# Modulation blocks of a two-block transformer kernel: eight products on four column tiles in one run, weights in four transfers of 512 KB

## The chip, the cores and the metric

The kernel runs on one core of a Trainium2 chip. The metric is the device time of one execution in microseconds (us). A kernel is profiled once on the chip; beside that there are plain runs with no profile.

Names of engines: PE is TensorE (matrix products), PEld its weight loads, DVE is VectorE, ACT is ScalarE, POOL is GpSimd, SP is the engine that issues nearly all DMA transfers here. Each engine works its own list of instructions strictly in order.

## The reference

Two blocks are computed on a sequence of 256 tokens of width 1024 in float32. The first has two layers of attention and a gated feed-forward with a short convolution. The second has two layers as well, a latent stream (`x`) and a context stream (`ctx`), and each of its layers is modulated by vectors that come from a conditioning vector. The change concerns only how these vectors are made:

```python
s_lat = jax.nn.silu(c)[:, None, :]
s_ctx = jax.nn.silu(c_ctx)[None, None, :]
for i in range(DEPTH):                                   # DEPTH = 2
    ml = jnp.split(s_lat @ w_ada[i] + b_ada[i], 6, axis=-1)
    mc = jnp.split(s_ctx @ w_ada[i] + b_ada[i], 6, axis=-1)
    ...
    u_lat = modulate(h_lat, g_pre_mix[i], ml[0], ml[1])  # rms_norm * (1 + scale) + shift
```

`w_ada` is 2 x 1024 x 6144 in float32, 50.3 MB in all, and is read once. Both vectors go through it together.

## The kernel before

**How the work is laid out.** Most products are split in two halves of reduced precision (`whi`, `wlo` for weights, `ah`, `al` for activations), and three products take the place of one: hi by hi, hi by lo, lo by hi. A weight goes DRAM to `raw` (SP), `raw` to `whi` (ACT), `raw` minus `whi` to `wlo` (DVE or POOL), and PE uses both. The modulation is the exception: its products are plain float32 and read the loaded weight as it is.

**The lanes.** Work is recorded in three lanes with buffers of their own: the latent lane `lat`, the context lane `cx` and the side lane `sd`. A scheduler then merges them into one list per engine by its own estimate of when each instruction is ready, and packs the buffers into the on-chip memory. So the lanes interleave on PE and on SP, and the order of the source is not the order on the engine.

**The modulation.** `ada` computes layer `i`'s vectors in 12 blocks of 512 columns, 24 blocks in all. A block sums over 1024 rows, that is over eight slabs of 128 rows by 512 columns. The left operand `self.sT[:, k]` has 32 columns (two of them used: latent and context), so a product writes only 32 of the 128 rows of a PSUM bank, and the product of slab `k` goes to rows 32*(k mod 4) onward. These four places are the four column tiles. The four partial sums are added at the end: the bank is copied out (`asb`), transposed in four pieces (`adaT`) and reduced on DVE.

```python
for kb in range(0, 8, a):
    raw = (L.big if a == 2 else L.mid)([128, a, 512], name="adaw")
    nc.sync.dma_start(raw, self.plain_rows(w)(kb, a, nb * 512, 512))
    for k in range(kb, kb + a):
        j = k % 4
        nc.tensor.matmul(ps[32 * j:32 * j + 32], self.sT[:, k], raw[:, k - kb], start=k < 4, stop=k >= 4)
```

**Who calls it.** `context1` makes blocks 0 to 3 of layer 0 in the context lane and `second_block` blocks 10 and 11 of layer 1, both with `a = 2` (four transfers of 512 KB). `rest` makes blocks 4 to 11 of layer 0 and `side` blocks 0 to 9 of layer 1, both in the side lane with `a = 1` (eight transfers of 256 KB). The side lane has one PSUM bank (`PS[3]`), which holds first a block's products and then its transposes.

**What sets the order.** Each product waits only for its own slab, so the scheduler may put other lanes' products between two slabs of a block. SP issues transfers in the order of its list; a transfer into a buffer that is still in use waits, and all behind it wait too.

Of the kernel before, what the change touches and what calls it, by code (L numbers as in the profile page):

```python
# [22 lines left out]

LAT = {"big": 10, "mid": 12, "small": 24, "raw": 4, "whi": 4, "wlo": 4, "uv": 3, "gC": 1}
CTX = {"cf": 1, "big": 8, "mid": 12, "small": 24, "raw": 4, "whi": 3, "wlo": 3, "wide": 8, "gC": 1}
SIDE = {"big": 2, "mid": 6, "small": 4}
LAT_NAMED = {"AR": "raw", "BK": "big", "G": "whi", "BKt": "wlo", "lw": "big", "kn": "big", "sq": "big", "bv": "big",
             "T": "big", "TT": "big", "TTr": "big", "Y": "big", "sy": "big", "sg": "mid", "v": "mid", "uv": "uv",
             "xs": "mid", "gC": "gC"}
# [157 lines left out]
class Net:  # L187
# [10 lines left out]
    def pools(self, ctx):  # L198
# [6 lines left out]
        self.cx = Lane(self, "cx", CTX, CTX_NAMED, (("C", PS[2]), ("C", PS[2])), 512)  # L205
        self.sd = Lane(self, "sd", SIDE, {}, (("D", PS[3]), ("D", PS[3])), 512)
        self.lat.open(ctx)
# [538 lines left out]
                self.last = nc.tensor.matmul(acc[t][n], hl[:, k, c], wh[:, n], start=False, stop=en)  # L746


    def ada(self, L, i, a, blocks=range(12)):

        self.mark(f"ada{i}")
        nc, I = self.nc, self.I
        if not self.adac:
            th = L.small(16, name="ath")
            nc.scalar.activation(th[:, 0:8], self.col("c", 0, 8), AF.Tanh, scale=0.5)
            nc.scalar.activation(th[:, 8:16], self.col("cc", 0, 8), AF.Tanh, scale=0.5)
            self.sT = self.keep([128, 8, 32], F32, name="sT")
            nc.gpsimd.memset(self.sT, 0.0)  # L760
            for s, n in ((0, "c"), (1, "cc")):
                v = th[:, 8 * s:8 * s + 8]
                nc.vector.scalar_tensor_tensor(v, v, 1.0, self.col(n, 0, 8), op0=OP.add, op1=OP.mult)
                nc.vector.tensor_scalar(self.sT[:, :, s], v, 0.5, None, op0=OP.mult)
        w = I["w_ada"][i]
        if len(self.adac) == i:
            self.adac.append(self.keep([128, 2, 48], F32, name=f"adac{i}"))
        ac = self.adac[i]
        for nb in blocks:
            ps = L.pA("ada")  # L770
            for kb in range(0, 8, a):
                raw = (L.big if a == 2 else L.mid)([128, a, 512], name="adaw")
                nc.sync.dma_start(raw, self.plain_rows(w)(kb, a, nb * 512, 512))
                for k in range(kb, kb + a):
                    j = k % 4
                    nc.tensor.matmul(ps[32 * j:32 * j + 32], self.sT[:, k], raw[:, k - kb], start=k < 4, stop=k >= 4)  # L776
            sb = L.mid([128, 512], name="asb")
            nc.scalar.activation(sb, ps, AF.Copy)

            ps = L.pA("adaT")  # L780
            for c in range(4):
                nc.tensor.transpose(ps[:, c * 128:(c + 1) * 128], sb[:, c * 128:(c + 1) * 128], self.ident)
            at = ac[:, :, 4 * nb:4 * nb + 4]
            nc.vector.tensor_reduce(at, ps.rearrange("p (c j r) -> p r c j", j=4, r=32)[:, 0:2], axis=AX.X, op=OP.add)  # L784
            nc.vector.tensor_tensor(at, at, self.col(f"b_ada{i}", 4 * nb, 4)[:, None].to_broadcast([128, 2, 4]),
                                    op=OP.add)
            if nb in (3, 9):
                at, n = (8, "gpm") if nb == 3 else (32, "gpf")
                for s in range(2):
                    nc.vector.scalar_tensor_tensor(ac[:, s, at:at + 8], ac[:, s, at:at + 8], 1.0,  # L790
                                                   self.col(f"{n}{i}", 0, 8), op0=OP.add, op1=OP.mult)
            if nb in (5, 11):
                at, n = (16, "g_post_mix") if nb == 5 else (40, "g_post_ff")
                pr = L.pA("adaR")
                for s in range(2):
                    nc.tensor.transpose(pr[:8, s * 128:(s + 1) * 128], ac[:, s, at:at + 8], self.ident)
                gp = L.mid([8, 128], name="gp")
                nc.gpsimd.dma_start(gp, I[n][i].rearrange("(c f) -> c f", f=128))
                rows = L.mid([8, 2, 128], name="arows")
                nc.vector.tensor_tensor(rows, pr[:8, 0:256].rearrange("c (s f) -> c s f", s=2),  # L800
                                        gp[:, None].to_broadcast([8, 2, 128]), op=OP.mult)
                ar = self.dr.tile([2, 1024], F32, name=f"arow{i}{at}")
                nc.gpsimd.dma_start(ar[:].rearrange("s (c f) -> c s f", f=128), rows)
                self.arow[i, at] = ar
            yield
            self.mark(f"ada{i}")
# [242 lines left out]
        nc.gpsimd.memset(self.state, 0.0)  # L1049

    def rest(self):
        for _ in self.ada(self.sd, 0, 1, range(4, 12)):
            pass

    def side(self):
        for _ in itertools.chain(self.ada(self.sd, 1, 1, range(10)), self.setup_odd(self.sd)):
            pass

    def behind(self, steps):

        with self.tc.issue_after(self.last.ins):
            for _ in steps:
                pass
# [517 lines left out]

    def context1(self):
        L = self.cx
        for _ in self.ada(L, 0, 2, range(4)):
            pass
        self.ctx_act = self.even_mix(L, 1, self.load_x(L, self.I["ctx"][0]))

# [129 lines left out]
    def second_block(self, x):  # L1717
        L = self.lat
        end = self.last
        act = self.even_mix(L, 0, x)  # L1720
        self.lat_out(0, act, x)
        odd = self.context2(end)
        self.lat_mlp(0, x)
        self.behind(odd)
        act = self.odd_mix(x)
        self.lat_out(1, act, x)
        self.behind(self.ada(self.cx, 1, 2, range(10, 12)))
        self.lat_mlp(1, x)


def run(tc, I, out, colw, cstw, keep):
    nc = tc.nc
    with ExitStack() as ctx:
        net = Net(tc, I)
        net.pools(ctx)
        net.setup(colw, cstw, keep)
        x = [net.keep([128, D], F32, name=f"x{t}") for t in range(2)]
        for t in range(2):
            nc.sync.dma_start(x[t], I["x"][0, t * 128:(t + 1) * 128])
        act=net.first_norm(0, x)  # L1740
        net.setup_first()
        net.setup_second()
        net.context1()
        net.first_layer(0, x, act)
        net.conv_ffn(0, x)
        net.rest()
        act1=net.first_norm(1, x)
        net.first_layer(1, x, act1)
        net.side()
        net.conv_ffn(1, x)  # L1750
        net.second_block(x)
        net.store_x(x, out[0])
# [38 lines left out]
```

## Time and profile before

| | us |
|---|---|
| median of three runs (2096.21 to 2100.75) | 2096.55 |
| the profiled execution | 2103.6 |
| its span, first to last instruction | 2101.5 |
| PE busy in it | 1940.0 (92%) |
| DVE, ACT, POOL busy | 1342.9, 1016.8, 926.6 |
| the modulation's products on PE, 192 of them (384 records, two for each) | 93.7 busy |

A product in plain float32 leaves two records on PE, so x2 in a row of the timeline below is one product and x16 are eight. Busy time is the union of the records: products that run side by side count once. Matmuls overlap at their ends, so the time that a product holds PE is read from the start of one to the start of the next.

### The profile page before, as it was taken

What the parts mean: (1) busy time and instruction counts of PE and PEld (TensorE: products, weight loads), DVE (VectorE), ACT (ScalarE), POOL (GpSimd) and SP (SyncE); (2) the same over time, 40 slices, a digit from 0 to 9 for tenths busy, and PEclk for the clock granted to TensorE, in tenths of its full rate; (3) what the DMA queues carried; (4) which work ended last, traced back from release to release, by engine and by line L of the source; (5) the groups of instructions that cost most, each with busy time, mean ns of one, the idle gap of its engine ahead of it and who ended that gap; (6) DMA issues with size and microseconds to landing.
All of it is one profiled execution on the core that took longest, in us unless ns stands there. A gap on an engine that the chain in (4) does not pass through costs nothing. (4 is left out here: it accounts for less than half of the span.)

```text
span 2101.5 us, 37449 instructions
## 1 busy us (share of the span) xinstructions
PE 1940.0 (92%) x14178; PEld 1629.7 (78%) x14178; DVE 1342.9 (64%) x2751; ACT 1016.8 (48%) x1942; POOL 926.6 (44%) x621
## 2 busy tenths in 40 slices
PE   5989999989998989999898998997699989998998
PEld 3667868988675458899797788897599978776997
DVE  4475377875687646687668888446864468656444
ACT  4355555544454434455556553333554454655443
POOL 3234544593232354344544455455244545113453
PEclk9999999999899999999999998998899999998999
DMA  9856554545354665566572334436465536234562
GB/s 335 288 188 208 175 168 153 162 148 175 115 188 162 220 191 165 171 192 200 142 234 91 106 98 138 139 117 188 153 192 191 191 100 218 66 116 142 189 197 74
DMA packets 270811, 351.04 MB, mean 167 GB/s; under 512 B 43150, under 2 KB 195469, under 8 KB 270632
## 3 DMA queue, kind: packets, MB, share of 16 engines
q1 hardware_dynamic: 267992, 343.32, 51.4%
q0 software_dynamic: 1968, 4.33, 0.7%
q8 instruction: 111, 1.82, 0.4%
q10 hardware_dynamic: 672, 1.02, 0.1%
q14 instruction: 68, 0.56, 0.1%
HBM read 334.04 MB, written 14.55 MB: 166 GB/s over the span
## 5 line engine op out<-in xcount | busy, mean ns | idle before, releaser
L267 POOL TENSOR_TENSOR wlo<-raw,whi 128x1024 fp32r<-128x1024 f32 (+2 forms) x408 | 777.6, 1920 | 982.7 <-ACT whi L263 834.2
L263 ACT ACTIVATE whi<-raw 128x1024 fp32r<-128x1024 f32 (+2 forms) x600 | 507.5, 882 | 156.7 <-PE prj L292 38.5
L267 DVE TENSOR_TENSOR wlo<-raw,whi 128x1024 fp32r<-128x1024 f32 x192 | 303.3, 1580 | 110.3 <-ACT whi L263 106.2
L306 PE MATMUL f<-ah,whi 128*128 128x256 f32 x768 | 223.6, 292 | 9.9 <-ACT whi L263 9.9
L308 PE MATMUL f<-ah,wlo 128*128 128x256 f32 x768 | 224.1, 292 | 4.2 <-POOL wlo L267 4.2
L307 PE MATMUL f<-al,whi 128*128 128x256 f32 x768 | 222.5, 290 | 0.0
L745 PE MATMUL acc<-wlo,hh 128*128 128x512 f32 x432 | 169.8, 393 | 0.0
L744 PE MATMUL acc<-whi,hh 128*128 128x512 f32 x432 | 167.1, 393 | 0.7 <-ACT hh L459 0.7
L746 PE MATMUL acc<-whi,hl 128*128 128x512 f32 x432 | 165.4, 391 | 0.0
L306 PEld LDWEIGHTS f<-ah,whi 128*128 128x128 f32 x768 | 151.4, 197 | 13.5 <-ACT whi L263 10.7
L308 PEld LDWEIGHTS f<-ah,wlo 128*128 128x128 f32 x768 | 151.2, 197 | 7.5 <-POOL wlo L267 4.9
L307 PEld LDWEIGHTS f<-al,whi 128*128 128x128 f32 x768 | 151.2, 197 | 1.8 <-DVE al L381 0.3
L1552 DVE TENSOR_TENSOR r<-r 128x512 f32<-128x512 f32 x48 | 40.8, 849 | 130.9 <-ACT r L1551 128.4
L1551 ACT ACTIVATE r<-f 128x512 f32<-128x512 f32 x48 | 28.7, 598 | 193.4 <-PE f L308 193.4
L290 PE MATMUL prj<-whi,ah 128*128 128x512 f32 (+1 forms) x272 | 110.7, 411 | 0.4 <-DVE bt L497 0.4
L291 PE MATMUL prj<-wlo,ah 128*128 128x512 f32 (+1 forms) x272 | 108.4, 399 | 0.6 <-DVE wlo L267 0.6
L292 PE MATMUL prj<-whi,al 128*128 128x512 f32 (+1 forms) x272 | 107.2, 401 | 1.4 <-DVE al L381 1.4
L776 PE MATMUL ada<-adaw,kept 128*32 128x512 f32 x384 | 93.7, 620 | 14.5 <-DMA adaw<-in_w_ada_dram 12.2
L308 PE MATMUL g<-ah,wlo 128*128 128x256 f32 x352 | 101.8, 289 | 4.8 <-POOL wlo L267 4.8
L306 PE MATMUL g<-ah,whi 128*128 128x256 f32 x352 | 101.3, 288 | 0.6 <-DVE kept L784 0.6
L308 PE MATMUL up<-ah,wlo 128*128 128x256 f32 x352 | 100.3, 285 | 1.4 <-POOL wlo L267 1.4
L307 PE MATMUL g<-al,whi 128*128 128x256 f32 x352 | 101.3, 288 | 0.0
(469 smaller groups left out, 4919.8 us busy)
## 6 DMA issues: line engine op xcount, KB each, us to landing
raw<-in_w_ff_dram SPq DMA_DIRECT2D x128, 512.0 KB, 3.9
raw<-in_w_up_dram SPq DMA_DIRECT2D x88, 512.0 KB, 4.7
adaw<-in_w_ada_dram SPq DMA_DIRECT2D x144, 256.0 KB, 4.8
raw<-in_w_ff_dram SPq DMA_DIRECT2D x128, 256.0 KB, 3.6
raw<-in_w_in_dram SPq DMA_DIRECT2D x48, 512.0 KB, 4.9
raw<-in_w_down_dram SPq DMA_DIRECT2D x44, 512.0 KB, 4.4
adaw<-in_w_ada_dram SPq DMA_DIRECT2D x24, 512.0 KB, 7.5
raw<-in_w_out_dram SPq DMA_DIRECT2D x24, 512.0 KB, 4.0
```

The lines of the kernel that those rows point to most:

```text
L263: nc.scalar.activation(hi, raw, AF.Copy)
L267: eng.tensor_tensor(lo, raw, hi.bitcast(F32), op=OP.subtract)
L290: nc.tensor.matmul(ps[t][:, :n], ah, wh[:, k], start=st, stop=False)
L291: nc.tensor.matmul(ps[t][:, :n], ah, wl[:, k], start=False, stop=False)
L292: self.last = nc.tensor.matmul(ps[t][:, :n], al, wh[:, k], start=False, stop=en)
L306: nc.tensor.matmul(pv[:, j], wh[:, k % a, c], ah, start=first, stop=False, skip_group_check=skip)
L307: nc.tensor.matmul(pv[:, j], wh[:, k % a, c], al, start=False, stop=False, skip_group_check=skip)
L308: nc.tensor.matmul(pv[:, j], wl[:, k % a, c], ah, start=False, stop=k == 7, skip_group_check=skip)
L744: nc.tensor.matmul(acc[t][n], hh[:, k, c], wh[:, n], start=st, stop=False)
L745: nc.tensor.matmul(acc[t][n], hh[:, k, c], wl[:, n], start=False, stop=False)
L746: self.last = nc.tensor.matmul(acc[t][n], hl[:, k, c], wh[:, n], start=False, stop=en)
L776: nc.tensor.matmul(ps[32 * j:32 * j + 32], self.sT[:, k], raw[:, k - kb], start=k < 4, stop=k >= 4)
```

## The change

The loads of a block come first, always as four transfers of two slabs; the products follow, and each is tied behind the one before it, at raised priority, so that the scheduler sees them as a chain. They start with the pair of slabs that was loaded last. The parameter `a` goes. The side lane gets six buffers of 4 KB a partition in place of two, and no longer loads into its 2 KB buffers.

```diff
-SIDE = {"big": 2, "mid": 6, "small": 4}
+SIDE = {"mid": 6, "small": 4, "big": 6}
...
-    def ada(self, L, i, a, blocks=range(12)):
+    def ada(self, L, i, blocks=range(12)):
...
-            for kb in range(0, 8, a):
-                raw = (L.big if a == 2 else L.mid)([128, a, 512], name="adaw")
-                nc.sync.dma_start(raw, self.plain_rows(w)(kb, a, nb * 512, 512))
-                for k in range(kb, kb + a):
-                    j = k % 4
-                    nc.tensor.matmul(ps[32 * j:32 * j + 32], self.sT[:, k], raw[:, k - kb], start=k < 4, stop=k >= 4)
+            raws = []
+            for kb in range(0, 8, 2):
+                raws.append(L.big([128, 2, 512], name="adaw"))
+                nc.sync.dma_start(raws[-1], self.plain_rows(w)(kb, 2, nb * 512, 512))
+
+            order = [6, 7, 4, 5, 2, 3, 0, 1]
+            self.run([lambda k=k, m=m: nc.tensor.matmul(ps[32 * (m % 4):32 * (m % 4) + 32], self.sT[:, k],
+                                                        raws[k // 2][:, k % 2], start=m < 4, stop=m >= 4)
+                      for m, k in enumerate(order)])
...
+    def run(self, products):
...
+        last = products[0]()
+        for p in products[1:]:
+            with self.tc.issue_after(last.ins), self.tc.high_priority():
+                last = p()
+        return last
...
-        for _ in self.ada(L, 0, 2, range(4)):
+        for _ in self.ada(L, 0, range(4)):
```

The calls in `rest`, `side` and `second_block` change in the same way.

What this does on PE, at the seventh block of `side` (layer 1), while the first block's second layer runs: `ada` is the block's bank, `om`, `S` and `PT` are attention products of the latent lane. Before:

```order
L776 MATMUL ada<-adaw,kept 32x512
L645 MATMUL om<-pt,v 64x256
L646 MATMUL om<-pt,v 64x128
L526 MATMUL S<-kT,qa 128x128
L527 MATMUL S<-kT,qa 128x256
L526 MATMUL S<-kT,qb 128x128
L527 MATMUL S<-kT,qb 128x256
L776 MATMUL ada<-adaw,kept 32x512
L541 MATMUL PT<-kept,L 128x128
L645 MATMUL om<-pt,v 64x256
L646 MATMUL om<-pt,v 64x128
L542 MATMUL PT<-kept,L 128x128
```

The rest of that block follows in three more pieces. The same block in the changed kernel, where `P` are small products of the context lane's recurrent scan:

```order
L1389 MATMUL P<-uv,G 32x64 x4
L1397 MATMUL P<-uv,BKt 64x64 x4
L777 MATMUL ada<-adaw,kept 32x512 x8
L1370 MATMUL P<-uv,G 64x64 x8
L1374 MATMUL P<-kept,AR 64x64 x8
L785 MATMUL adaT<-kept,asb 128x128 x4
```

The eight products stand as one row. Over the whole list of PE there are 65 such stretches before (51 of one to four products, 14 of five to nine) and 27 after: 19 of eight, one of sixteen (two blocks end to end), and seven pieces of 5, 3, 1, 7, 5, 2 and 1 products, into which three blocks of the first 100 us still fall.

On SP, in the first 100 us, `raw` of `w_in` are weights of the first layer, `toep` and `bias` the tables of its attention, `xc` the context stream. Before:

```order
L773 DMA adaw<-in_w_ada_dram 128x512 x2
L498 DMA toep<-bt 128x4x256
L261 DMA raw<-in_w_in_dram 128x2x512
L498 DMA toep<-bt 128x4x256
L773 DMA adaw<-in_w_ada_dram 128x2x512 x8
L560 DMA bias<-toep 128x256
L1476 DMA xc<-in_ctx_dram 128x1024 x2
L261 DMA raw<-in_w_in_dram 128x2x512 x4
```

After:

```order
L774 DMA adaw<-in_w_ada_dram 128x2x512 x2
L261 DMA raw<-in_w_in_dram 128x2x512
L498 DMA toep<-bt 128x4x256
L774 DMA adaw<-in_w_ada_dram 128x2x512 x10
L560 DMA bias<-toep 128x256
L774 DMA adaw<-in_w_ada_dram 128x2x512 x2
L261 DMA raw<-in_w_in_dram 128x2x512 x3
L1488 DMA xc<-in_ctx_dram 128x1024 x2
L261 DMA raw<-in_w_in_dram 128x2x512
```

More of the modulation's weights stand ahead of the same rows. Ahead of the first weight of the next projection (the `raw` x4 before, the `raw` x3 after) there are 12 MB of them before (16 transfers of 256 KB and 16 of 512 KB) and 19 MB after (38 of 512 KB), MB taken as 1024 KB.

## Rows read from the trace of the kernel before

**Rows 1.** The page: busy time by engine, and the granted clock in 40 slices.
```profile
PE 1940.0 (92%) x14178; PEld 1629.7 (78%) x14178; DVE 1342.9 (64%) x2751; ACT 1016.8 (48%) x1942; POOL 926.6 (44%) x621
PEclk9999999999899999999999998998899999998999
```
**Rows 2.** Stretch, length; PE, PEld, DVE, ACT, POOL busy; clock; DMA share; GB/s.
```profile
0.00:105.00 105.00, 80.22 (x370) 51.26 (x374) 48.47 (x136) 42.01 (x74) 31.57 (x27) 0.97 0.90 311
105.00:330.00 225.00, 211.59 (x1277) 165.24 (x1270) 138.43 (x383) 125.03 (x297) 106.57 (x80) 0.97 0.57 185
550.00:800.00 250.00, 230.10 (x1433) 152.86 (x1432) 163.23 (x442) 108.58 (x232) 88.83 (x97) 0.95 0.54 176
```
**Rows 3.** The same for instructions on tile ada alone: PE, PEld, ACT.
```profile
0.00:105.00 105.00, 18.15 (x88) 3.07 (x92) 2.88 (x5) 0.97 0.90 311
105.00:330.00 225.00, 24.70 (x108) 3.67 (x100) 4.18 (x7) 0.97 0.57 185
550.00:800.00 250.00, 47.04 (x160) 7.19 (x160) 5.98 (x10) 0.95 0.54 176
1880.00:2101.00 221.00, 3.85 (x32) 0.83 (x32) 1.17 (x2) 0.96 0.48 156
```
**Rows 4.** Timeline of PE: start, duration, what; modulation runs of one, two, three, eight.
```profile
25.52 0.39 PE L291 MATMUL prj<-wlo,ah 128*128 128x512 f32 x1
25.75 0.39 PE L292 MATMUL prj<-whi,al 128*128 128x512 f32 x1
26.07 1.04 PE L776 MATMUL ada<-adaw,kept 128*32 128x512 f32 x2
27.04 0.50 PE L290 MATMUL prj<-whi,ah 128*128 128x512 f32 x1
27.38 0.39 PE L291 MATMUL prj<-wlo,ah 128*128 128x512 f32 x1
...
28.17 1.05 PE L776 MATMUL ada<-adaw,kept 128*32 128x512 f32 x4
...
33.67 1.06 PE L776 MATMUL ada<-adaw,kept 128*32 128x512 f32 x6
...
104.17 1.92 PE L776 MATMUL ada<-adaw,kept 128*32 128x512 f32 x16
```
**Rows 5.** PE's waits over the whole run: who for whom, total, times, longest.
```profile
PE ada L776 <- DMA adaw<-in_w_ada_dram: 12.2, 6, 5.5
PE qT L420 <- DVE hn L399: 8.0, 2, 6.5
```
**Rows 6.** Timeline of PE around the longest of these waits (in brackets), and later.
```profile
657.09 2.65 PE L776 MATMUL ada<-adaw,kept 128*32 128x512 f32 x4 [5.49 <-DMA adaw<-in_w_ada_dram]
660.43 1.11 PE L782 MATMUL adaT<-kept,asb 128*128 128x128 f32 x4 [0.69 <-ACT asb L778]
661.34 1.06 PE L432 MATMUL kT<-kept,hn 128*128 128x128 f32 x4
662.05 0.78 PE L290 MATMUL prj<-whi,ah 128*128 128x512 f32 x1
...
664.76 0.46 PE L290 MATMUL prj<-whi,ah 128*128 128x512 f32 x1
...
690.69 5.19 PE L776 MATMUL ada<-adaw,kept 128*32 128x512 f32 x14
```
**Rows 7.** Busy time and clock in the stretch of rows 6.
```profile
657.00:665.00 8.00, 7.22 (x19) 4.34 (x20) 4.66 (x13) 1.29 (x2) 0.21 (x1) 0.51 0.61 202
```
**Rows 8.** DMA issues: count, size, median us from issue to landing.
```profile
adaw<-in_w_ada_dram SPq DMA_DIRECT2D x144, 256.0 KB, 4.8
adaw<-in_w_ada_dram SPq DMA_DIRECT2D x24, 512.0 KB, 7.5
```
**Rows 9.** SP's waits in the first 330 us, of those on the modulation.
```profile
SPq L773 <- PE ada L776: 13.4, 5, 7.8
SPq L1476 <- PE ada L776: 7.0, 2, 5.3
```

More of the change, by code (lines that the diff above doesn't have):

```diff
@@ L1051, in rest @@
     def rest(self):
-        for _ in self.ada(self.sd, 0, 1, range(4, 12)):
+        for _ in self.ada(self.sd, 0, range(4, 12)):
             pass
     def side(self):
-        for _ in itertools.chain(self.ada(self.sd, 1, 1, range(10)), self.setup_odd(self.sd)):
+        for _ in itertools.chain(self.ada(self.sd, 1, range(10)), self.setup_odd(self.sd)):
             pass
+    def run(self, products):
[4 more added lines that the diff above has]
+        return last
     def behind(self, steps):
@@ L1726, in second_block @@
         self.lat_out(1, act, x)
-        self.behind(self.ada(self.cx, 1, 2, range(10, 12)))
+        self.behind(self.ada(self.cx, 1, range(10, 12)))
         self.lat_mlp(1, x)
```

## The prediction

> **What bounds the kernel now.** I read the page first: PE is busy 92% of the span, no other engine over 64% (PEld apart, which works beside PE), and the granted clock stands near full in every slice [rows 1]. Then the table by stretches, which says where the modulation lies and how full PE is there. It lies in three stretches and a tail: 0 to 105 us, 105 to 330 us, 550 to 800 us, and two blocks near the end [rows 3]. PE is busy 211.6 of 225 us in the second and 230.1 of 250 in the third [rows 2]: 94% and 92%, with 13.4 and 19.9 us idle. In the first it waits at the start for data, and DMA is at 90% [rows 2]. So in two of three stretches PE is the bound by amount of work: three lanes are merged, and what PE drops, another lane's product can fill. The DMA share there is 0.57 and 0.54.
>
> Then the timeline, for what a product costs. One product alone takes 1.04 us, two in a row 1.05, three 1.06, eight 1.92 [rows 4]. Products on different column tiles thus run side by side, and a stretch of one costs as much as a stretch of four. That is the whole case for the change: the kernel before pays for 65 stretches where 24 would do.
>
> **The sum.** It is made against the profiled execution (2103.6 us, span 2101.5), which was 7.05 us over the median of the runs; I take the differences off the median, 2096.55.
>
> *A. Busy time of the products.* Before: 18.15 + 24.70 + 47.04 + 3.85 = 93.7 us [rows 3]. After, by the pieces that the order shows: 19 of eight at 1.92; two of 5 and one of 7, two rounds each, 1.92; 3, 1, 2, 1 products at 1.05; one of sixteen, 1.92 + 2 x 0.87 = 3.66, where 0.87 = 1.92 - 1.05 is a further round of four. Sum 36.5 + 5.8 + 4.2 + 3.7 = 50.2. Gain 43.5 us, of it some 14 before 330 us (13 blocks there now, where there were 12; 42.9 against 29) and 30 in the third stretch (nine blocks for ten). Part of the 93.7 is already stretching: the fourteen records at 690.69 take 5.19 us [rows 6] where rounds would take 1.92, since each product waited for its own slab.
>
> *B. Changing over.* Without the lone product the L291 after it would have started at 25.75 + 2 x 0.23 = 26.21, 0.23 being the step from 25.52 to 25.75; it started at 27.38 [rows 4]. So the stretch costs 1.17 us, 0.13 more than its busy time. 65 - 27 = 38 stretches fewer: gain 4.9 us.
>
> *C. Waits of PE for the slabs.* Before: 12.2 us in 6 waits, the longest 5.5 [rows 5]. They go, but others come. A run starts with the last slab, so it waits for all four transfers, in order, with every lane's products behind it. And of six buffers a block takes four, so the last two transfers of the next block are issued only once this block's run is over. None of this is in the trace; the ends are nothing (all loads early enough) and 24 x 5.5 = 132 us. A wait now is 12.2 / 6 = 2.0 us; I take one for every second block: 12 x 2.0 = 24.4. Net loss 12.2. I stay near the low end since nine runs in the 250 us of the third stretch stand 28 us apart on average, and a transfer of 512 KB of these weights, most of which go in the crowded first stretch now, lands 7.5 us after its issue [rows 8].
>
> *D. The first 100 us.* By the order 7 MB more of modulation weights go ahead of the next projection's weights and of the context rows. At 311 GB/s for a share of 0.90 [rows 2] DMA at full share moves 346 GB/s, so 7.3 million bytes take 21 us; DMA has 0.10 x 105 = 10.5 us to spare there. So up to 10.5 us of delay, and down to nothing if PE lives off what is already there. I take the middle, 5 us.
>
> *E. Everything else.* No product, copy or reduction is added or dropped; the evictions (asb, ACT) stay 24. SP issues 72 transfers for the 144 of 256 KB [rows 8]. The buffers' places and the order of later stretches change with the schedule; both signs are open, and I take nothing. The two last blocks already stood as x16 in the trace's tail (3.85 us for two, [rows 3]) and gain nothing.
>
> Sum: -43.5 - 4.9 + 12.2 + 5 = -31.2 us. On the profiled execution's own time 2072.4, on the median 2065.4. Cover: this counts PE time as span, which holds as long as other lanes have products ready; PE's idle 33.3 us in the two later stretches says that they mostly do. What is late next is the main chain of the first block (norms on DVE, the split of weights on ACT and POOL).
>
> **Rivals.**
>
> *The products were filler.* Where PE waits for the main chain (a qT product for head norms on DVE, 8.0 us in two waits [rows 5]), a lone modulation product costs nothing, and taking it away only makes PE idle. For: the 33.3 us idle in the two stretches show that chains do bind at places. Against: the stretches are busy over 90%, and the products were put between products of the main lane that wait for nothing [rows 4]. If two thirds of A and B is lost so, the gain is 48.4 / 3 = 16.1, less 5 of D (C at zero net): 11 us, 2085.5.
>
> *No new waits.* If all slabs are there in time and D is nothing, C turns to a gain of 12.2: -60.6 us, 2036.
>
> *Late slabs (slower).* Place: the head of each run in the second and third stretch. SP works in order; it already waits 13.4 us for modulation products to release a slab's buffer, and 7.0 more before the context rows [rows 9]. After the change such a wait of SP holds back a pair of large transfers and whatever weights stand behind; PE then stands at the head of the run. Price: a wait of 5.5 us, as the longest now, and after it PE comes back at a lower clock: from 662.05 to 664.76 six products of the projection (five of their rows left out) start 0.45 us apart [rows 6] where 0.23 is the step at full clock [rows 4], and the transposes before them took 0.71 to the next start; the granted clock of 657 to 665 us is 0.51 [rows 7], about the lower of the two levels, 1.2 GHz. That is 6 x 0.22 = 1.3 us lost by the six, and with half of the transposes' 0.71 some 1.6. Nine blocks x 7.1 and four side blocks in the second stretch x 5.5 make 86 us of loss; against the best gain of 60.6 and with D's 5 that is +30 us, 2127. It decides once new waits pass 55.6 us, 2.3 us for each of 24 blocks. Against it: six buffers let two transfers of the next block go early. The Trainium skill has a rule that speaks on this side ("TensorE: Matmul & The Clock Gate", section "HAM oscillation — how this bites in real kernels"): where each burst of products is shorter than the wait for its data, PE starts every burst at the low clock. By that rule every late run would pay the 1.6 us, 22 side-lane and context runs together 35 us; by the rows only a run that has waited several us does. The trace agrees for the one long wait.
>
> That the change does not do what it says is only partly so, and counted in A: three blocks of the first 100 us are still cut.
>
> **How the numbers follow.** Chances: the forecast 0.54, filler 0.17, no new waits 0.13, late slabs 0.16. A measurement of this kernel can't tell less than about 0.2% (4.2 us) from no change. Faster by more than that: 0.54 + 0.13 + 0.13 of filler's 0.17 (at its centre 11 us) = 0.80. Filler's other 0.04 and 0.01 of late slabs end within it: 0.05. Slower: 0.15. Range: the low end takes the no-waits case almost to its 2036, and leaves out 0.06: 2040. The high end takes in filler and the no-change band's lower part and leaves out 0.14: 2096. The forecast's own range is 2048 to 2083, from C between zero and twice what I took and D between its ends.
>
> **What would show it.** Right: the busy time of ada falls from 93.7 to 50 us, with runs of eight at 1.92 us; the rest of the first block comes earlier by some 30 us, which the start of the second block's first products in the timeline shows; PE's waits on adaw are near 25 us; PE's busy time falls by 43 to 45 us and its idle time stays within 15 us of what it is. Wrong: waits on adaw over 55 us, with stretches of granted clock near 0.5 behind them (late slabs); or PE's idle time grown by 30 us or more in 105 to 330 and 550 to 800 us on norms and splits (filler). For D: the first products of the context stream later than now while DMA is at its limit past 105 us. The whole forecast falls if the later stretches, from 800 us on, which the change does not touch, turn out longer or shorter by more than 15 us.

## The result, and the profile after

The changed kernel took 2161.91 us (median of 4 runs, 2155.34 to 2165.85), the kernel before 2097.07 beside it (2096.21 to 2100.75). The ratio is 1.0301, 95% interval 1.0276 to 1.0326: slower by 64.8 us, where I had forecast 31 us less. The profiled execution took 2165.85, its span 2164.1.

First the modulation itself, as in [rows 3]: stretch and length, then PE, PEld and ACT busy on tile `ada`, granted clock, DMA share, GB/s.

```profile
0.00:105.00 105.00, 15.70 (x96) 2.98 (x96) 3.59 (x6) 0.95 0.97 344
105.00:330.00 225.00, 13.26 (x112) 3.02 (x112) 3.56 (x6) 0.95 0.58 188
330.00:550.00 220.00, 0.00 (x0) 0.00 (x0) 0.00 (x0) 0.89 0.39 116
550.00:800.00 250.00, 20.18 (x144) 4.11 (x144) 5.62 (x10) 0.88 0.54 172
1880.00:2164.00 284.00, 3.85 (x32) 0.83 (x32) 1.18 (x2) 0.97 0.44 135
```

The sum is 53.0 us in place of 93.7: what the change set out to do, it does. Now the page, which answers to [rows 1]:

```profile
PE 1947.7 (90%) x14178; PEld 1667.6 (77%) x14178; DVE 1365.7 (63%) x2751; ACT 1026.3 (47%) x1942; POOL 891.8 (41%) x621
PEclk9999999888979888999999999799889999998999
```

PE is busy 7.7 us longer, not 43 shorter. So all its other products together take 1894.7 us where they took 1846.3, 48 us more for the same products. The clock row shows a part of it: nine slices with an 8 and two with a 7, where five had an 8.

To see where the end moved, I read five stages off PE's timelines: the start of the first network's first `g` product, the time from it to the last `acc` product, the middle from there to the second network's first `g` (the second layer's attention and scan), the second network in the same way, and the rest (second block) to the last `acc` of all. In us:

| kernel | start | 1st network | middle | 2nd network | rest | banks for `g`, `up` |
|---|---|---|---|---|---|---|
| before | 292 | 247 | 241 | 233 | 1079 | 2 |
| after | 295 | **323** | 256 | 194 | 1087 | **1** |

The five differences, +3, +76, +15, -39 and +8, make the 63 us by which the trace is longer. The first network is the place. In it PE waits as follows (290 to 620 us; who for whom: total, times, longest):

```profile
PE g L306 <- DVE cu L700: 12.2, 3, 4.2
PE acc L744 <- ACT hh L459: 10.2, 1, 10.2
PE acc L745 <- POOL wlo L267: 5.8, 2, 2.9
PE up L306 <- DVE cu L700: 5.3, 1, 5.3
```

None of the four stood in the kernel before in that stretch. `g` is the gate's product, and `cu` is what DVE makes of the previous `up`: a gate waits until the bank of the `up` before it has been read out. The network works through eleven units. In the kernel before, `up` starts in every unit before DVE has read its `g` out; in the changed kernel it starts only after that in the third to ninth, and products on `acc` stand between the two. So in these units `g` and `up` share one PSUM bank, where they had one each.

The waits are not all of it. The first network as a whole, before and after (length; PE, PEld, DVE, ACT, POOL busy; clock, DMA share, GB/s):

```profile
292.00:539.00 247.00, 238.28 (x1906) 210.15 (x1902) 176.11 (x260) 126.44 (x215) 137.24 (x105) 0.99 0.48 151
295.00:618.00 323.00, 283.00 (x2188) 249.50 (x2187) 200.73 (x358) 134.68 (x232) 129.75 (x104) 0.89 0.39 118
```

PE's idle time grows from 8.7 to 40.0 us. The other 45 us are busy time: 282 more records, of work that ran later before, and all of them at a mean granted clock of 0.89 in place of 0.99.

The source asks for nine banks (`PS` is 4, 2, 2, 1), and the packer lays some over others by when they are in use. What held the other bank stands in the timeline of the changed kernel (start, duration, what):

```profile
183.84 1.93 PE L777 MATMUL ada<-adaw,kept 128*32 128x512 f32 x16
...
625.68 0.72 ACT L361 ACTIVATE xn<-kept,rstd 128x512 f32<-128x512 f32 x1 [2.16 <-DVE rstd L347]
628.04 0.72 ACT L361 ACTIVATE xn<-kept,rstd 128x512 f32<-128x512 f32 x1 [1.64 <-DVE rstd L347]
628.67 0.58 ACT L781 ACTIVATE asb<-ada 128x512 f32<-128x512 f32 x1
...
629.69 1.06 PE L785 MATMUL adaT<-kept,asb 128*128 128x128 f32 x4
```

The first block of `side` makes its eight products at 183.84 us and is copied out at 628.67. For 445 us its bank is held. Its copy-out `asb` needs a 2 KB buffer of the side lane, and these are handed out in the order of the source, where the four rows `xn` of the second layer's norm come before it. They are written only after the first network. In the kernel before, the slabs came out of the same 2 KB buffers, behind `xn` too, so the products could not run ahead of their copy-out: the first product of `side` came at 551 us. The change moved the slabs to the 4 KB buffers, which are not behind `xn`. The products got out, the copy-out did not.

### The profile page after: what moved, and what is told of

It is laid out like the page before. It is cut to its first block, busy times and chain, and to the rows that moved or that the text cites. A ratio compares the mean times of both kernels' runs of the same rounds, so it can differ in the third digit from the quotient of the medians.

```text
span 2164.1 us, 37356 instructions
## 1 busy us (share of the span) xinstructions
PE 1947.7 (90%) x14178; PEld 1667.6 (77%) x14178; DVE 1365.7 (63%) x2751; ACT 1026.3 (47%) x1942; POOL 891.8 (41%) x621
## 4 chain that ended last, share of the span: by engine, by line
PE 66%; DVE 19%; DMA 4%; issue 4%; ACT 3%; POOL 3%; SPq 0%; DVEq 0%; ACTq 0%; POOLq 0%
PE acc L745 4%; PE acc L746 4%; PE acc L744 4%; PE f L307 3%; PE f L306 3%; PE f L308 3%; PE prj L291 2%; PE prj L290 2%; PE prj L292 2%; PE up L306 2%; PE up L308 2%; PE up L307 2%; POOL wlo L267 2%; PE g L306 2%; PE g L308 2%
## 5 line engine op out<-in xcount | busy, mean ns | idle before, releaser
L267 POOL TENSOR_TENSOR wlo<-raw,whi 128x1024 fp32r<-128x1024 f32 (+2 forms) x408 | 752.0, 1853 | 1094.5 <-ACT whi L263 976.2
L263 ACT ACTIVATE whi<-raw 128x1024 fp32r<-128x1024 f32 (+2 forms) x600 | 519.1, 886 | 415.6 <-PE f L307 96.7
L267 DVE TENSOR_TENSOR wlo<-raw,whi 128x1024 fp32r<-128x1024 f32 x192 | 258.0, 1344 | 258.0 <-ACT whi L263 255.6
L306 PE MATMUL f<-ah,whi 128*128 128x256 f32 x768 | 221.9, 290 | 10.5 <-ACT whi L263 10.5
L306 PE MATMUL g<-ah,whi 128*128 128x256 f32 x352 | 108.3, 308 | 13.4 <-DVE cu L700 12.2
L1564 DVE TENSOR_TENSOR r<-r 128x512 f32<-128x512 f32 x48 | 94.0, 1959 | 36.6 <-ACT r L1563 36.5
L308 PE MATMUL g<-ah,wlo 128*128 128x256 f32 x352 | 106.6, 303 | 3.3 <-POOL wlo L267 3.3
L306 PE MATMUL up<-ah,whi 128*128 128x256 f32 x352 | 102.4, 291 | 5.3 <-DVE cu L700 5.3
L307 PE MATMUL g<-al,whi 128*128 128x256 f32 x352 | 106.0, 301 | 0.3 <-DVE al L376 0.3
L744 PEld LDWEIGHTS acc<-whi,hh 128*128 128x128 f32 x432 | 81.4, 189 | 28.5 <-ACT hh L459 12.7
L307 PE MATMUL up<-al,whi 128*128 128x256 f32 x352 | 101.7, 289 | 0.0
```

Source lines behind the costliest of these rows:

```text
L263: nc.scalar.activation(hi, raw, AF.Copy)
L267: eng.tensor_tensor(lo, raw, hi.bitcast(F32), op=OP.subtract)
L306: nc.tensor.matmul(pv[:, j], wh[:, k % a, c], ah, start=first, stop=False, skip_group_check=skip)
L307: nc.tensor.matmul(pv[:, j], wh[:, k % a, c], al, start=False, stop=False, skip_group_check=skip)
L308: nc.tensor.matmul(pv[:, j], wl[:, k % a, c], ah, start=False, stop=k == 7, skip_group_check=skip)
L744: nc.tensor.matmul(acc[t][n], hh[:, k, c], wh[:, n], start=st, stop=False)
```

## The experiments

Theories: *held bank* (above); *six large buffers* (16 KB less for the other lanes, or earlier loads in the way); *runs put first* (a run ahead of the main chain). Later *filler* (PE's time in the modulation is worth nothing) and *new order* (any other order of the same work costs something). Times are medians; the ratio is to the kernel before on the same chip.

**e1, e2: let the bank go in two ways.**

```diff
e1      net.conv_ffn(0, x)
+       net.ffn_end = net.last
        net.rest()
    def side(self):
+       with self.tc.issue_after(self.ffn_end.ins):
            for _ in itertools.chain(self.ada(self.sd, 1, range(10)), ...
e2 (first_norm's call of the norm: its rows from the main lane)
-       rows=self.sd if i else None
+       rows=None
```

> The changed kernel with one addition: on TensorE the side lane's work for layer 1 stands behind the last product of the first layer's feed-forward. Loads of 512 KB, runs of eight and the six buffers stay. Theory 'held bank': in the changed kernel the first layer-1 block ran its products at 184 us, its copy-out came only at about 630 us, and the PSUM bank held between left the first feed-forward one bank for its two halves (g and up), so it took 323 us (first g to last acc) where it took 247. Then this kernel's first feed-forward takes 240 to 260 us, and the time is 2060 to 2095 us. Rival 'six large buffers': they squeeze the weights' buffers; feed-forward about 320 us, time 2145 to 2170. Rival 'runs put first': unbroken runs at raised priority disturb the main lane; time 2145 to 2170.

> The changed kernel with the four row buffers of the second layer's first norm taken from the latent lane, not from the side lane's 2 KB buffers. Theory 'held bank': the copy-out of the first layer-1 block waited because it takes a 2 KB buffer of the side lane in the order of the source, behind those four rows, which are written only after the first feed-forward. With the rows elsewhere the copy-out follows the products, no bank is held, the first feed-forward has two banks again: it takes 240 to 290 us (layer-1 blocks may now run inside it), time 2050 to 2095 us. Both rivals (six large buffers; runs put first): 2145 to 2170.

e1 2126.99, ratio 1.0116 (1.0093 to 1.0140); e2 2116.31, 1.0067 (1.0043 to 1.0091). The first network is back at 253 and 255 us, with two banks. Against the 1.0301 of the change this gives back 1.85% and 2.34%, 39 and 49 us. But both stay above the kernel before, and my range for either had its top at 2095: the held bank is more than half of the loss, not all of it, and the gain of 31 us is still missing.

**e3, e4: make the loss without the change.** e3 gives the 256 KB loads of the kernel before a tag of their own, e4 makes `g` and `up` of the first network take turns in one bank, with no other edit.

```diff
e3
-SIDE = {"big": 2, "mid": 6, "small": 4}
+SIDE = {"big": 2, "mid": 6, "small": 4, "aw": 8}
-                raw = (L.big if a == 2 else L.mid)([128, a, 512], name="adaw")
+                raw = (L.big(...) if a == 2 else L.tile("aw", [128, a, 512], F32, "adaw"))
e4 (first network only; the same for "up")
-                    L.pB("g")
+                    self.ps.tile([128, 512], F32, name="g", tag="E", bufs=1)
```

> The kernel before with one edit: the side lane's loads of 256 KB go to eight 2 KB buffers of their own, not to the buffers that the norm's rows share. No run, no 512 KB loads in the side lane. Theory 'held bank': layer-1 products now start early as in the changed kernel, a bank is held through the first feed-forward, which takes 300 us or more; time 2130 to 2175 us. Both rivals: nothing of theirs is in it; 2085 to 2110.

> The kernel before with one edit: in the first layer's feed-forward the two halves g and up take turns in one PSUM bank; the second layer's keeps two. The modulation is as before. Theory 'held bank': this alone costs what the change cost, first feed-forward 300 us or more, time 2130 to 2175 us. If one bank is not the price, 2090 to 2110.

e3 2181.54, ratio 1.0393 (1.0359 to 1.0426): a bank is held from before the first network to its end (products at 225.57 us, copy-out at 650.77), and the network takes 336 us. e4 2205.34, ratio 1.0486 (1.0457 to 1.0514): the network takes 385 us. Both times lie over the 2130 to 2175 that I expected, e4's by 30 us. PE's waits in that network, e3:

```profile
PE acc L744 <- ACT hh L459: 12.5, 1, 12.5
PE g L306 <- DVE cu L700: 11.9, 3, 4.3
```

and e4 (its later lines stand three lower):

```profile
PE g L306 <- DVE cu L703: 20.8, 3, 9.3
PE acc L748 <- POOL wlo L267: 15.5, 2, 7.9
```

The same `g` behind `cu`: in e4 with products and loads untouched, in e3 with the loads only sent to other buffers. So one bank for two is the cause of the long first network. Its net price is less than 76 us, since the context's work done meanwhile is missing from the second network (194, 198, 198 us in the three kernels with one bank, 221 to 249 in all others): in the changed kernel 76 - 39 = 37 us, where e1 and e2 gave back 39 and 49. The Trainium skill ("Perfetto Trace Analysis", section "Optimizing Tensor Performance") says that independent groups of products should rotate through different PSUM banks, so that copying one out overlaps the next; these runs agree, 323 to 385 us against 244 to 264.

**e5: PE's time cut, nothing else of the change.**

```diff
-  nc.tensor.matmul(ps[32 * j:32 * j + 32], self.sT[:, k], raw[:, k - kb], ...
+  nc.tensor.matmul(ps[32 * j:32 * j + 32, 0:128], self.sT[:, k], raw[:, k - kb, 0:128], ...
```

> The kernel before, with each of the 192 products of the modulation over 128 of its 512 columns (its loads, buffers and copy-outs stay; the other three quarters of each block are left out and filled with the first), so some 60 us of PE's time go and nothing else of the change is in it. It asks what PE's time in these products is worth. 'PE time is the bound' (as my sum had it): 2030 to 2060 us. 'Filler' (PE waits there for the main chain anyway, and the clock falls with it): 2075 to 2100, with PE's idle time between 550 and 800 us grown by 25 us or more.

2114.81, ratio 1.0069 (1.0049 to 1.0090): slower, though the modulation takes 40.0 us of PE in place of 93.7. Neither theory's range holds it. Its middle is 254 us, not 241.

**e6 to e8: runs and buffers apart.**

```diff
e6, e7
-SIDE = {"big": 2, "mid": 6, "small": 4}
+SIDE = {"big": 2, "mid": 14, "small": 4}
e7 (products of a block as the change's chain, from 256 KB loads)
+  raws = [... eight slabs ...]
+  self.run([... eight products ...])
e8 (the buffers of the kernel before)
+  for h in range(0, 8, 4):
+      raws = [... the four slabs of the half ...]
+      self.run([... four products ...])
```

> The kernel before, products and 256 KB loads as they are, with 14 in place of 6 buffers of 2 KB in the side lane: 16 KB more memory, as much as the change takes, and loads that may go earlier. 'Memory' (the 16 KB cost the other lanes their places, or the earlier loads hold up the first 100 us): 2110 to 2125. 'Filler': no difference beyond 10 us, 2090 to 2107. 'PE time is the bound': 2090 to 2105 as well, as no product is taken away.

> The kernel of e6_more_mid_buffers with each block as one run of eight on four column tiles, from loads of 256 KB: the runs without the six large buffers, and without a block whose copy-out is held for 400 us. To be read against e6. 'PE time is the bound': 35 us or more under e6. 'Filler': within 15 us of e6. If it is near 2120 where e6 is near 2100, the runs themselves cost something that neither theory has.

> The kernel before with its own buffers and loads, and the products chained within each half of a block: two runs of four for each block (1.06 us each, so some 51 us for 24 blocks in place of 94). No buffer is added, no load is made larger, and a run waits for four slabs of 256 KB, which the six buffers hold. 'PE time is the bound': 2055 to 2070. 'Filler': 2080 to 2105. Above 2110 would say that chained runs do harm by themselves.

e6 2123.40, ratio 1.0112 (1.0062 to 1.0163); e7 2156.27, 1.0266 (1.0236 to 1.0295); e8 2150.38, 1.0245 (1.0219 to 1.0270). e6 was what the memory theory expected. e7 and e8 went past every range. The modulation's line of e7 over the whole run (busy, mean of one):

```profile
L775 PE MATMUL ada<-adaw,kept 128*32 128x512 f32 x384 | 104.9, 677 | 8.8 <-DVE kept L784 6.5 <-DMA adaw<-in_w_ada_dram 2.3
```

The products take longer than in the kernel before, not less (100.7 us in e8), because neither kernel has the runs that I expected of it. Where the kernel before has 65 stretches and the changed one 27, e7 has 74 and e8 76. One block of e7 on PE (start, duration, what; the first two stretches run at the lower clock):

```profile
656.92 2.46 PE L775 MATMUL ada<-adaw,kept 128*32 128x512 f32 x4 [0.88 <-DMA adaw<-in_w_ada_dram]
660.83 2.54 PE L775 MATMUL ada<-adaw,kept 128*32 128x512 f32 x4 [1.45 <-DMA adaw<-in_w_ada_dram]
668.10 1.05 PE L775 MATMUL ada<-adaw,kept 128*32 128x512 f32 x2
669.45 1.05 PE L775 MATMUL ada<-adaw,kept 128*32 128x512 f32 x4
670.69 1.05 PE L775 MATMUL ada<-adaw,kept 128*32 128x512 f32 x2
```

Other products still stand inside the chains. So e7 and e8 do not set runs and buffers apart, and e8's sign for harm by chained runs (above 2110) shows none: whether its 50 us are the chains' or a new order's, these two can't tell.

**e9 to e12: what PE's time is worth.** Each product made twice in the kernel before (e9) and in e1 (e10), over a quarter of its width in e1 (e11); e12 has the mends of e1 and e2 together. e10 repeats the four products of each half of a run, not each product by itself.

```diff
e9, e10
-  matmul(..., start=first, stop=last)
+  for r in range(2): matmul(..., start=first and r == 0, stop=last and r == 1)
-  nc.scalar.activation(sb, ps, AF.Copy)
+  nc.scalar.activation(sb, ps, AF.Copy, scale=0.5)
e11 (in e1, as e5)
-  matmul(ps[...], self.sT[:, k], raws[k // 2][:, k % 2], ...
+  matmul(ps[..., 0:128], self.sT[:, k], raws[k // 2][:, k % 2, 0:128], ...
```

> The kernel before, with each product of the modulation made twice into the same bank (the sum is halved in the copy-out, so the output stays): some 55 us more of PE's time, nothing else. 'PE time is the bound': 2145 us or more. 'Filler, and a new order costs 10 to 25 us by itself' (which e5 and e6 suggest): 2105 to 2130.

> The kernel of e1_hold_back with each run made twice: runs of sixteen, some 40 us more of PE's time, about what the kernel before spends. 'PE time is the bound': 35 us or more over e1's 2127, 2160 or more. 'Filler': within 15 us of e1, 2110 to 2142.

> The kernel of e1_hold_back with each product over 128 of its 512 columns (the other three quarters of each block are left out and filled with the first): some 35 us less of PE's time. 'PE time is the bound': 2090 to 2100. 'Filler': within 15 us of e1, 2112 to 2142.

> The change with both mends at once: the side lane's second half held back to the end of the first feed-forward network (e1) and the norm's rows from the main lane's buffers (e2). No bank is held. 'PE time is the bound' would have the change's 40 us now: 2060 to 2075. 'Filler, and a new order costs 10 to 25 us': 2105 to 2130, as e1 and e2.

e9 2170.80, ratio 1.0331 (1.0315 to 1.0347); e10 2115.03, 1.0071 (1.0051 to 1.0090); e11 2099.36, 0.9983 (0.9964 to 1.0001); e12 2109.77, 1.0046 (1.0029 to 1.0063). The modulation over the whole run, in e11:

```profile
0.00:2098.00 2098.00, 18.93 (x384) 10.87 (x384) 14.26 (x24) 0.94 0.53 167
```

in e1:

```profile
0.00:2123.00 2123.00, 53.55 (x384) 11.28 (x384) 14.21 (x24) 0.95 0.53 165
```

and in e10:

```profile
0.00:2112.00 2112.00, 93.47 (x768) 24.04 (x768) 14.21 (x24) 0.96 0.53 166
```

With 40 us more of PE's time e10 is 12 us faster than e1; with 35 us less e11 is 28 us faster. From e11 to e10, 75 us of PE's time cost 16. The four do not agree. e10 and e12 came out where *filler* had them. e9 and e11 came out where *PE time is the bound* had them: e9 has 165.8 us of modulation, 72 more than the kernel before, and is 70 us longer, and e11 lies inside the 2090 to 2100 of that theory and 13 us under *filler*'s range. So these runs give PE's time no price that holds for the whole kernel. Each of them also has an order of its own, and what that costs is the next question.

**e13 to e16: a new order of the same work.**

```diff
e13 (reaches only the context lane's six blocks, two slabs to a load)
-                for k in range(kb, kb + a):
+                for k in reversed(range(kb, kb + a)):
e14
-SIDE = {"big": 2, "mid": 6, "small": 4}
+SIDE = {"big": 2, "mid": 7, "small": 4}
e15 (in e1)
-            order = [6, 7, 4, 5, 2, 3, 0, 1]
+            order = list(range(8))
e16 (in e1)
-SIDE = {"mid": 6, "small": 4, "big": 6}
+SIDE = {"mid": 6, "small": 4, "big": 5}
```

> The kernel before, with the two products of each 512 KB load in the context lane's six blocks made in the other order: the same work, the same buffers, the same loads, and 2911 of the rows of PE's order stand elsewhere. It prices a new order. 'A new order costs 10 to 25 us by itself': 2108 to 2130. 'The change's remaining loss is its own (loads, buffers)': 2095 to 2106.

> The kernel before with 7 in place of 6 buffers of 2 KB in the side lane: 2 KB more memory, the same products and loads, another order. 'A new order costs 10 to 25 us by itself': 2108 to 2130. 'The change's remaining loss is its own': 2095 to 2106.

> The kernel of e1_hold_back with the slabs in the order of their loads (0 to 7) in place of last load first: the same work in another order. 'A new order moves the time by 10 to 25 us': anywhere in 2098 to 2130, as e1 (2127) and e12 (2110) are. If last-first matters by itself, 10 us or more under the lowest of these.

> The kernel of e1_hold_back with five large buffers in place of six: 4 KB less memory, one load less ahead. 'A new order moves the time': 2098 to 2130. 'Six large buffers squeeze the other lanes': under 2100.

e13 2115.69, ratio 1.0084 (1.0057 to 1.0110); e14 2147.25, 1.0220 (1.0198 to 1.0242); e15 2122.67, 1.0098 (1.0060 to 1.0137); e16 2153.87, 1.0247 (1.0217 to 1.0277). e13 and e14 compute what the kernel before computes with the same loads, and lose 17 and 49 us; e14 and e16 went past the 2130 that I gave a new order. PE is busy as before in e13 (it has the 1942.5 us, [rows 1] 1940.0):

```profile
PE 1942.5 (92%) x14178; PEld 1630.2 (77%) x14178; DVE 1358.6 (64%) x2751; ACT 1018.2 (48%) x1942; POOL 925.7 (44%) x621
```

So a new order (in e14 with one buffer more) is worth as much as the change could be. e16 gives no sign that the six large buffers are to blame, since with five the kernel is slower; but its 27 us over e1 are within what an order moves, so it does not rule them out as a part of the rest. The stages of all these kernels:

| kernel | start | 1st network | middle | 2nd network | rest | banks |
|---|---|---|---|---|---|---|
| e1 | 293 | 253 | 242 | 236 | 1089 | 2 |
| e2 | 309 | 255 | 241 | 221 | 1082 | 2 |
| e3 | 304 | 336 | 240 | 198 | 1088 | 1 |
| e4 | 285 | 385 | 240 | 198 | 1078 | 1 |
| e5 | 279 | 249 | 254 | 235 | 1085 | 2 |
| e6 | 301 | 251 | 241 | 221 | 1088 | 2 |
| e7 | 305 | 251 | 256 | 249 | 1085 | 2 |
| e8 | 308 | 256 | 239 | 244 | 1091 | 2 |
| e9 | 312 | 264 | 255 | 235 | 1095 | 2 |
| e10 | 297 | 244 | 245 | 232 | 1084 | 2 |
| e11 | 289 | 246 | 232 | 235 | 1086 | 2 |
| e12 | 297 | 253 | 236 | 232 | 1087 | 2 |
| e13 | 286 | 246 | 238 | 247 | 1087 | 2 |
| e14 | 285 | 248 | 275 | 239 | 1083 | 2 |
| e15 | 290 | 247 | 239 | 238 | 1085 | 2 |
| e16 | 307 | 254 | 254 | 239 | 1087 | 2 |

## Why the prediction was wrong

**The step that failed first: "E. Everything else ... I take nothing".** I named the buffers' places and the order of later stretches, called both signs open, and left them out of the sum and of the rivals. The held bank is such a change of places: +37 us net, shown by undoing it (e1, e2) and by making it without the change (e3, e4). It could have been read beforehand: `PS` asks for nine banks that are laid over one another, and in PE's order `up` of the first network's third to ninth units stood behind products on `acc` that came after its `g`, as in no unit of the kernel before.

**The step that failed second: the cover, "this counts PE time as span, which holds as long as other lanes have products ready".** I took PE at 92 to 94% busy for a bound by amount of work, so that each us of products would be a us of span. The middle stage shows that there it is not one. In the kernel before, the middle (539 to 780 us) holds 47 us of the modulation; PE, PEld, ACT on `ada`, then all engines (PE, PEld, DVE, ACT, POOL):

```profile
539.00:780.00 241.00, 47.04 (x160) 7.19 (x160) 5.98 (x10) 0.94 0.57 183
```

```profile
539.00:780.00 241.00, 217.18 (x1317) 140.78 (x1316) 162.20 (x454) 104.38 (x226) 85.69 (x93) 0.94 0.57 183
```

In e2 all blocks but the two near the end are made before it, and its middle (564 to 805 us) holds none:

```profile
564.00:805.00 241.00, 0.00 (x0) 0.00 (x0) 0.00 (x0) 0.83 0.37 107
```

```profile
564.00:805.00 241.00, 211.61 (x1319) 163.85 (x1317) 165.60 (x447) 101.76 (x230) 93.69 (x101) 0.83 0.37 107
```

Both take 241 us. Where the 47 us went: the other products' records grew from 1157 to 1319, context work moved up from the second network (which is 12 us shorter), and they took 212 us in place of 170 at a mean granted clock of 0.83 in place of 0.94 (1 is the upper level, 2.4 GHz). By their number alone they would take 194 us, an estimate that counts all records alike; the rest of the growth goes with the lower clock. So PE looks nearly as busy without the 47 us as with them. The same shows in more kernels: with 0, 8.2, 22.5, 41.6 and 47.0 us of modulation (e2, e11, e1, e10, before) the middle takes 241, 232, 242, 245 and 241 us. In e2 the work was moved, not taken away, and it was not free where it went: the start holds 45.85 us of modulation in place of 38.55, with DMA at 0.84 in place of 0.71, and takes 309 us in place of 292.

PE's longest waits in the middle are 9.2 and 5.9 us in e2, and 5.5 and 5.0 in the kernel before. The Trainium skill has a rule that waits for data between bursts bring the clock down, which the prediction weighed for late slabs ("TensorE: Matmul & The Clock Gate", section "HAM oscillation — how this bites in real kernels"). These rows agree with its direction. Which wait of the main chain sets the 241 us I have not shown. Over the changed kernel's whole run the largest is `nT` on the norm's rows `xn`, 42.5 us in 13 (37.6 in 8 before), and the next is this one, up from 8.0 [rows 5]:

```profile
PE qT L420 <- DVE hn L399: 14.7, 3, 8.3
```

The other steps:

- *A, busy time of the products* was right: 53.0 us for 50.2. Two runs of eight at a lower granted clock (0.61 and 0.50) make the difference: 3.08 and 3.64 us in place of 1.92. What the 41 us are worth in time is not shown: e10 and e11 differ by 16 us for 75, e1 and e11 by 28 for 35, both within what an order moves.
- *B, changing over* falls with the cover: it is PE time as well, and no run shows it apart.
- *C, waits for slabs* was wrong in size: I took 24.4 us of new waits; the list of PE's waits now holds none on `adaw`, and the view of the tile 0.7 us in two. The pairs come early enough.
- *D, the first 100 us*, had the right mechanism: DMA is at 0.97 in them, for 0.90 before, at 344 GB/s, and the context's rows are issued 15 us later (108.39 us, 92.99 before) and first read 11 us later (117.85, 106.69 before). The first network starts at 295 us, not earlier than 292, although PE has 28.96 us of modulation before it where it had 38.55. If PE's time counts there, D took 12 us, for the 5 that I put in and the 10.5 of its upper end. e6 starts at 301 with products as before, so part of it can be order.

Of the rivals, *filler* named what the middle shows, at a chance of 0.17 and with a third of the gain left, and I argued it away by the busy share. It had no place for the held bank, and its sign did not come: PE's idle time in the two stretches of [rows 2] grew by 22.6 us (busy 201.36 and 217.66 us there now), not by 30. *Late slabs* had the right sign by a mechanism that did not happen. My list of signs said that the forecast falls if the stretches from 800 us on move by more than 15 us. The second network, most of which lies there, moved by 39, but it got shorter; the loss stands before it, so this sign came true by luck. The range was miscounted too: with 0.15 for slower its upper end, 2096, cannot leave out only 0.14.

**What remains.** The changed kernel stands 64.8 us above the kernel before, and the trace's 63 divide into 37 the held bank, +15 the middle, +8 the rest, +3 the start. The last three are of the size that a new order costs by itself: middle 232 to 275 and rest 1078 to 1095 over the sixteen other kernels, of which none was measurably faster than the kernel before, twelve of them 0.5 to 2.7% slower. So the order is the likely cause of these 26 us, but that is argued from their size. Which places in the order cost it is open, and so is what became of the 31 us of gain.

## What to carry to other kernels

A change in where loads land changes what may run ahead of what. Before pricing an edit, ask for every resource that it fills (here a PSUM bank) what must happen before it is given back, and whether that step is now behind something that the first step is no longer behind.

A busy share of 92% does not show a bound by amount of work. Read the granted clock and the number of records beside it, and cut the work to a quarter, or double it, in more than one kernel: of e9 to e12 two fitted such a bound and two did not. And where a scheduler merges lanes, swap two equal products first: 17 us, and 49 for one spare buffer, is the noise that a gain of 31 has to stand out from.

## What the runs showed that I had not expected

The same DVE instruction of the second block, 48 times, takes 849 ns in the kernel before:

```profile
L1552 DVE TENSOR_TENSOR r<-r 128x512 f32<-128x512 f32 x48 | 40.8, 849 | 130.9 <-ACT r L1551 128.4 <-issue 2.2
```

and 1959 ns in the changed one, of the same shape and type:

```profile
L1564 DVE TENSOR_TENSOR r<-r 128x512 f32<-128x512 f32 x48 | 94.0, 1959 | 36.6 <-ACT r L1563 36.5
```

It is as long in e1, e2, e11, e12, e15 and e16 (1927 to 1982) and as short in the other ten. The mean hides two kinds. One of them in the changed kernel, beside the POOL instruction that makes a `wlo` at the time:

```profile
1641.96 2.39 POOL L267 TENSOR_TENSOR wlo<-raw,whi 128x1024 fp32r<-128x1024 f32 x1 [3.15 <-ACT whi L263]
1642.40 2.50 DVE L1564 TENSOR_TENSOR r<-r 128x512 f32<-128x512 f32 x1 [0.70 <-ACT r L1563]
```

and one in the kernel before, where POOL's comes after it:

```profile
1648.06 0.69 DVE L1552 TENSOR_TENSOR r<-r 128x512 f32<-128x512 f32 x1 [4.31 <-ACT r L1551]
1651.39 2.49 POOL L267 TENSOR_TENSOR wlo<-raw,whi 128x1024 fp32r<-128x1024 f32 x1 [5.38 <-ACT whi L263]
```

The long one ends 0.55 us after POOL's instruction. In the changed kernel 31 of the 48 meet such a `wlo`, and they take 2.47 to 2.52 us; in the kernel before 3 do. In all eighteen kernels an `r` with nothing of POOL's beside it takes 0.64 to 0.72 us. So what a new order changed is whether `r` meets POOL. That POOL holds it up is read from this coincidence; no run moves one of them alone. The kernel is not late by it: the idle time before `r` fell from 130.9 to 36.6 us.
